# Two more weight parts of the second feed-forward layer by adding transfers, and three more turns of zeros at the start

## The chip, the cores and the metric

The kernel runs on one core of a Trainium2 chip. A core has a matrix engine (TensorE, PE in the profile, with its weight loads as PEld), a vector engine (VectorE, DVE), a scalar engine (ScalarE, ACT), a general engine (GpSimd, POOL) and a sync engine (SyncE, SP) that here only issues transfers. Each engine takes its instructions in the order in which they were written, and waits for other engines at semaphores. The metric is the device time of one execution in microseconds.

## The reference

One residual block over 512 positions of width 1024, all in float32:

```python
h = h + 0.5 * _swiglu(_rmsnorm(h, ffn1_norm[i]), ffn1_w_in[i], ffn1_w_out[i])
z = _rmsnorm(h, mix_norm[i]) @ w_in[i]
...
h = h + jnp.concatenate([y_conv, y_gla], axis=-1) @ w_out[i]
h = h + 0.5 * _swiglu(_rmsnorm(h, ffn2_norm[i]), ffn2_w_in[i], ffn2_w_out[i])
gate = jax.nn.sigmoid(_rmsnorm(h, ple_norm[i]) @ ple_w_gate[i])
h = h + gate * (p[i] @ ple_w_proj[i])
```

`_swiglu` splits `x @ w_in` into a gate and an up half, 2816 columns each, and returns `(silu(gate) * up) @ w_out`. The change lies in the second of these feed-forward layers, and in the first microseconds of the program.

## The kernel before

Activations are kept transposed, as tiles of 128 features by 512 positions. Every float32 product is made of three products of a shorter format: each operand is split into a high part (a cast, names that end in H, or wh for weights) and a lesser part, what the cast left out (names in L, or wl). PE then computes high by high, high by lesser and lesser by high into one bank of PSUM.

**How a weight tile gets its two parts.** A load of 512 KB, issued by SP, fills one of six raw buffers (wr). Then `high` (line 183) casts it on ACT into wh. The lesser part is made in one of two ways. `low` (line 193) is one subtraction on DVE, wl = wr - wh. `added` (line 198) leaves DVE out: ACT copies the tile with a factor of -1 into wl, and POOL issues a transfer that adds wr to it. What is written as `p.part(name)` is `high` and `low`; `p.add_part(name)` is `high` and `added`, where wl first takes minus the high part:

```python
        h3, l3, r3 = w
        act.mul(l3, r3, -1.0)
        pool.dma_start(out=l3.bitcast(F32), in_=r3, accum_op=ALU.add)
```

The profile's row for the multiplication is an ACT ACTIVATE `wl<-wr`, and for the transfer a POOL DMA `wl<-wr`. There are six buffers each for wh and wl.

**The feed-forward layer.** `ffn` (line 604) handles the 22 blocks of 128 gate and up columns as eleven pairs. Pair 0 is computed plainly ahead of the layer's plan. For each other pair the 2 by 2 arrangement of its weights (a11, a12, a21, a22) is multiplied in seven products instead of eight, on sums of the weights (s1 to s4, made by DVE) and of the activations (t1 to t4). The seven are the units m1, m2, m6, m7, m5, m4 and m3, each of 24 matmuls of 128x256. A pair's units take the operands a11, a12, s2, s3, s1, a22 and s4 in that order. Several units add into the same bank of PSUM; where one of them needs the sum so far, ACT copies it out first (`snap`, rows `sq<-ps` and `u<-ps`), and the next unit that adds to this bank must wait for the copy. So unit m5 of a pair can only begin once ACT has copied out what m6 left (`p.u2`, row `u<-ps`).

**What sets the order.** The units stand in one list, and `drive` (line 584) goes through it. Each unit has preparations with a distance: a preparation of distance 4 (`AHEAD`) is written four units ahead of the unit that needs it, ahead of that unit's matmuls; loads have 7 or 9. Between the units stand the pieces of the layer's second product with `w_out`. Where the second layer begins, the list reads: m1, m2 of pair 1, m1 of pair 2, then m6, m7, m5 of pair 1, m2 of pair 2, m4 and m3 of pair 1, m6, m7, m5 of pair 2, m1 and m2 of pair 3, a piece of `w_out`, m4 and m3 of pair 2. PE, DVE and ACT are held to the written order here; the gating (bank plus copy, times the row factor, silu on ACT, product on DVE: rows u, g, s, m) is written behind the unit that ends it.

**The start.** `warm_up(n)` (line 140) has PE turn (transpose) the identity n times into a bank that nobody reads; the document calls these turns of zeros after the change's name for them. Ten stand ahead of the turn of the first gain vector (`turn_vec`, row `ax<-ident,vcol1r`), and four between the turn of the first 128 columns of x (`turn_x(0)`, row `ps<-ident,x`) and the first real products (`ps<-hgH,wh`). The spare bank (ax) is a single one: the gain vector's turn waits until the last of the ten has ended, and the four wait until DVE has copied the gain vector out.

Of the kernel before, what the change touches and what calls it, by code (L numbers as in the profile page):

```python
# [62 lines left out]
def block_kernel(ctx: ExitStack, tc: tile.TileContext, a: dict, out: bass.AP):  # L63
# [32 lines left out]
    def bank():  # L96
        return pp.tile([P, SEQ], F32, tag="mm", bufs=7, name=nm("ps"))

    def aux():
        return pp.tile([P, SEQ], F32, tag="aux", bufs=1, name=nm("ax"))  # L100
# [15 lines left out]
    def columns(names, n, tile_name, queue):  # L116

        row = cp.tile([n, P], F32, name=tile_name + "r")
        col = cp.tile([P, n], F32, name=tile_name)
        r0 = 0  # L120
        for name, m in names:
            queue.dma_start(out=row[r0:r0 + m, :], in_=a[name][0].rearrange("(r p) -> r p", p=P))
            for c in range(m):
                vcols[name, c] = col[:, r0 + c:r0 + c + 1]
            r0 += m

        def turn():
            ps = aux()
            pe.transpose(ps[:, 0:n], row, ident[:n, :n])
            dve.tensor_copy(col, ps[:, 0:n])  # L130

        return turn
# [7 lines left out]
    def warm_up(n):  # L140
        idle = aux()
        for _ in range(n):
            pe.transpose(idle[:, 0:P], ident, ident)

    warm_up(10)
    turn_vec = columns(vecs[:1], 8, "vcol1", nc.scalar)

    def split(src, s, alloc=bt):
# [110 lines left out]
    def spread(col, copy=True):  # L259

        ps = aux()
        for j in range(TB):
            pe.transpose(ps[:, j * P:(j + 1) * P], col[:, j:j + 1].to_broadcast([P, P]), ident)
        if not copy:
            return ps
        bc = tmp("bc", bufs=1)
        act.copy(bc, ps)
        return bc
# [170 lines left out]
    hg, xps, xt, squares = [], [], {}, []  # L439
# [12 lines left out]
    def turn_x(c):  # L452
        ps = bank()
        for t in range(TB):
            pe.transpose(ps[:, t * P:(t + 1) * P], xt[c][t], ident)
        xps.append(ps)
# [63 lines left out]
        nc.sync.dma_start(out=made[2][i * RANK:(i + 1) * RANK, :], in_=a["gate_w_up"][0])  # L520
    turn_vec()
    turn_x(0)
    warm_up(4)
    ps0 = [bank() for _ in range(4)]
    split_w(0, 1, dve.tensor_copy)
    split_x(0)
    mid = []
# [22 lines left out]
    xb = Right(hg, "ffn1_norm")  # L550
# [31 lines left out]
    AHEAD = 4  # L582
# [18 lines left out]
        for f in left:  # L601
            f()

    def ffn(w_in, w_out, x, gname, given, first, rsb, hooks, plain):


        norm = Norm()
# [93 lines left out]
        def plain_unit(j):  # L701

            up, i, k = j // 4, j // 2 % 2, j % 2
            def run(p):
                if not j:
                    p.g, p.s = {}, {}
                if not k:
                    p.x = bank()
                ps = p.x
                wh, wl = p.part(f"a{1 + up}{1 + k}")  # L710
                cs = slice(i * P, (i + 1) * P)
                for c in range(4):
                    mm3(ps, wh[:, c, cs], wl[:, c, cs], *x.rows[4 * k + c], k == c == 0, k == 1 and c == 3)
                if not k:
                    return []
                if not up:
                    def gate():
                        p.s[i] = silu(scaled(ps, "g1"))
                    return [gate]
                return [lambda: gated_block(p, p.s[i], scaled(ps, "u1"), i),  # L720
                        lambda: act_parts(p) if i else None]
            return run
# [4 lines left out]
        def unit(kind, i):  # L727
            p = pairs[i]

            def go(run):  # L730
                left = run(p)
                hooks.get((kind, i), lambda *_: None)()
                return left

            if kind[0] == "h":
                j = int(kind[1])
                part, run = (f"a{1 + j // 4}{1 + j % 2}", plain_unit(j)) if j % 4 < 2 else (None, plain_unit(j))
                if part:
                    return [(AHEAD, lambda: p.part(part)), (9, lambda: p.fetch(part))], lambda: go(run)
            else:  # L740
                part, run = USES[kind]
            before = [(AHEAD + (kind == 'm5'), lambda: p.part(part))] if part else []
            if kind in ("m1", "m2"):
                before.append((7, lambda: p.fetch(part)))
            elif kind == "m6":
                before += [(9, lambda: p.fetch("a21", "a22")), (6, p.s12)]
            elif kind in ("m7", "m3"):
                before.append((6, p.s3_ if kind == "m7" else p.s4_))

            return before, lambda: go(run)  # L750
# [63 lines left out]
        def add(kind, i):  # L814
            if 0 <= i < npair and (kind, i) not in had:
                had.add((kind, i))
                units.append(unit(kind, i))
# [49 lines left out]
    w_in = a["w_in"][0]  # L867
    w_ahead = []

    def sums_hooks(x, names, at):  # L870

        h = {}
        for name, key in zip(names, at):
            h[key] = lambda *_, name=name: x.split(name)
        return h

    hooks = sums_hooks(xb, ("t2", "t3", "t1", "t4"), (("h5", 1), ("h7", 1), ("h3", 2), ("m1", 3)))
    hooks.update({("h%d" % (i + 1), 1): f for i, f in enumerate(steps[2:])})
    hooks.update({("m5", 3): lambda *_: made[0](), ("m5", 4): lambda *_: constants(),
                  ("m4", 10): lambda *_: w_ahead.append(ahead(w_in, D_CONV, 2 * P)),  # L880
                  ("last", 4): lambda *_: w_ahead.append(ahead(w_in, 0, 2 * P))})
    hg, norm = ffn(ffn1_in, a["ffn1_w_out"][0], xb, "mix_norm", {0: Left(ffn1_in, 0), 1: w1},
                   (ps0[:2], ps0[2:]), lambda: spread(mid[0]), hooks, (1, 2))
    pool.on = False
# [63 lines left out]
    mid = []  # L948
# [10 lines left out]
    rs, rsb = mid  # L959
# [358 lines left out]
    ffn2_in = a["ffn2_w_in"][0]  # L1318
    wf = {i: Left(ffn2_in, 2 * i) for i in range(3)}
# [41 lines left out]
    norm = Norm()  # L1361
# [57 lines left out]
    hg = nhg  # L1419

    def plain_block(p, up, i, mid={}):
        ps = bank()
        cs = slice(i * P, (i + 1) * P)
        for k in range(DC):
            if k in mid:
                mid[k]()
            wh, wl = p.part(f"a{1 + up}{1 + k // 4}")
            mm3(ps, wh[:, k % 4, cs], wl[:, k % 4, cs], *hg[k], k == 0, k == DC - 1)
        return ps

    mid = []
    xb = Right(hg, "ffn2_norm")
# [5 lines left out]
    g0 = plain_block(w0, 0, 0)  # L1438
    steps[1]()
    steps[2]()  # L1440
    u0 = plain_block(w0, 1, 0, {4: lambda: mid.append(norm.rows())})
# [4 lines left out]
    g1_ = plain_block(w0, 0, 1, {1: lambda: mid.append(spread(mid[0]))})  # L1446
# [5 lines left out]
    u1_ = plain_block(w0, 1, 1)  # L1452
# [3 lines left out]
    hooks = sums_hooks(xb, ("t4",), (("m2", 1),))  # L1456
# [63 lines left out]
    def todo(*fs):  # L1520
        return lambda *_: [f(*v) for f, *v in fs]
# [4 lines left out]
                  ("rest", 2): todo((q_high, b21, q21, 0), (first_sum, 0), (third_sum, 0)),  # L1526
                  ("rest", 4): todo((q_high, b21, q21, 1), (first_sum, 1), (third_sum, 1)),
                  ("rest", 6): todo((final_in,), (row_sums, 0))})
    hg, norm = ffn(ffn2_in, a["ffn2_w_out"][0], xb, "ple_norm", wf, ((g0, u0), (g1_, u1_)), mid[1], hooks, ())

# [143 lines left out]
    def kept(ps, name, **kw):  # L1676
        o = tmp(name, **kw)
        act.copy(o, ps)
        return o
# [23 lines left out]
    m1 = [kept(p_, "sq", bufs=3) for p_ in x_]  # L1703
# [98 lines left out]
```

## Time and profile before

| | us |
|---|---|
| median of three runs | 949.27 |
| the three runs | 949.77, 949.27, 948.17 |
| the profiled execution | 948.38 |
| its span, first to last instruction | 946.7 |
| PE busy in the span | 935.0 (99%) |
| DVE busy | 755.6 (80%) |
| ACT busy | 477.0 (50%) |
| POOL busy | 57.2 (6%) |

The span lies inside the profiled execution; 1.7 us of it are outside the first and last instruction. Starts in the rows are counted from the span's start. A row of the timeline gives start, duration, engine, line, operation, tiles and shapes, how many equal instructions follow each other, and in brackets the engine's idle time just ahead and what ended it. The line is nearly always L46, a helper that records every operation, so rows are told apart by their tiles; buffer numbers are left out there. Matmuls overlap: each is shown with 0.28 us or more, but they follow each other at a shorter distance, and it is this distance that counts.

In the second layer PE goes through a unit in 2.88 us, one matmul every 0.12 us. Before the change m6 of pair 2 starts at 586.23, m7 at 589.11, m5 at 593.10, m1 of pair 3 at 596.07, m2 of pair 3 at 598.95 and m4 of pair 2 at 607.30.

### The profile page before, as it was taken

What the parts mean: (1) busy time and instruction counts of PE and PEld (TensorE: products, weight loads), DVE (VectorE), ACT (ScalarE), POOL (GpSimd) and SP (SyncE); (2) the same over time, 40 slices, a digit from 0 to 9 for tenths busy, and PEclk for the clock granted to TensorE, in tenths of its full rate; (3) what the DMA queues carried; (4) which work ended last, traced back from release to release, by engine and by line L of the source; (5) the groups of instructions that cost most, each with busy time, mean ns of one, the idle gap of its engine ahead of it and who ended that gap; (6) DMA issues with size and microseconds to landing.
All of it is one profiled execution on the core that took longest, in us unless ns stands there. A gap on an engine that the chain in (4) does not pass through costs nothing.

```text
span 946.7 us, 14553 instructions
## 1 busy us (share of the span) xinstructions
PE 935.0 (99%) x5842; PEld 831.1 (88%) x5842; DVE 755.6 (80%) x1030; ACT 477.0 (50%) x720; POOL 57.2 (6%) x72
## 2 busy tenths in 40 slices
PE   9999999999999999999999999999999999999996
PEld 7888999999999988788877889899999999998885
DVE  5876887887788566999986788887878787866896
ACT  5652544434433574463564874444434433445882
POOL 0000200000000110001030020000000000000121
PEclk9999999999999999999999999999999999999998
DMA  7532323342323593346552572332243224347463
GB/s 229 180 114 72 106 69 117 105 131 80 103 90 111 140 257 83 81 102 167 134 126 77 154 163 82 112 114 88 90 134 112 67 91 133 96 147 225 89 113 110
DMA packets 107831, 113.43 MB, mean 120 GB/s; under 512 B 5155, under 2 KB 96469, under 8 KB 107764
## 3 DMA queue, kind: packets, MB, share of 16 engines
q1 hardware_dynamic: 101732, 94.67, 32.3%
q0 software_dynamic: 6016, 17.83, 10.4%
q8 instruction: 46, 0.75, 0.3%
q14 instruction: 21, 0.17, 0.1%
q10 hardware_dynamic: 16, 0.00, 0.0%
HBM read 93.61 MB, written 2.10 MB: 101 GB/s over the span
## 4 chain that ended last, share of the span: by engine, by line
PE 96%; DVE 2%; ACT 1%; issue 1%; POOLq 0%; POOL 0%; DVEq 0%; ACTq 0%
PE ps L46 94%; PE ax L46 2%; DVE wl L46 1%; DVE g L46 0%; ACT wh L46 0%; DVE u L46 0%; DVE wr L46 0%; ACT s L46 0%; DVE y L46 0%; DVE sm L46 0%; DVE actL L46 0%; DVE hgL L46 0%; ACT wl L46 0%; POOLq L1798 0%; ACT ycH L46 0%
## 5 line engine op out<-in xcount | busy, mean ns | idle before, releaser
L46 PE MATMUL ps<-hgH,wh 128*128 128x256 f32 (+1 forms) x768 | 235.9, 312 | 0.0
L46 PE MATMUL ps<-hgL,wh 128*128 128x256 f32 (+1 forms) x768 | 234.2, 310 | 0.0
L46 PE MATMUL ps<-hgH,wl 128*128 128x256 f32 (+1 forms) x768 | 234.0, 310 | 0.0
L46 DVE TENSOR_TENSOR wl<-wr,wh 128x1024 fp32r<-128x1024 f32 (+2 forms) x162 | 189.6, 1181 | 48.1 <-ACT wh L46 48.0
L46 ACT CAST wh<-wr 128x1024 fp32r<-128x1024 f32 (+2 forms) x177 | 177.8, 1019 | 39.8 <-PE ps L46 19.8
L46 PEld LDWEIGHTS ps<-hgH,wh 128*128 128x128 f32 x768 | 146.9, 192 | 9.9 <-issue 1.1
L46 PEld LDWEIGHTS ps<-hgH,wl 128*128 128x128 f32 x768 | 146.7, 191 | 7.8
L46 PEld LDWEIGHTS ps<-hgL,wh 128*128 128x128 f32 x768 | 146.3, 191 | 8.0 <-issue 0.2
L46 PE MATMUL ps<-actH,wh 128*128 128x512 f32 x352 | 137.4, 390 | 0.0
L46 PE MATMUL ps<-actL,wh 128*128 128x512 f32 x352 | 137.3, 390 | 0.0
L46 PE MATMUL ps<-actH,wl 128*128 128x512 f32 x352 | 136.9, 389 | 0.0
L46 ACT ACTIVATE s<-g 128x512 f32<-128x512 f32 x48 | 30.4, 633 | 190.2 <-DVE g L46 190.2
L46 DVE SCALAR_TENSOR_TENSOR cv<-glu,cw,cv 128x502 f32<-128x502 f32 (+24 forms) x120 | 81.0, 731 | 0.6
L46 PEld LDWEIGHTS ps<-actH,wl 128*128 128x128 f32 x352 | 66.1, 188 | 14.0
L46 PEld LDWEIGHTS ps<-actH,wh 128*128 128x128 f32 x352 | 66.2, 188 | 13.0
L46 PEld LDWEIGHTS ps<-actL,wh 128*128 128x128 f32 x352 | 66.2, 188 | 12.4
L46 DVE SCALAR_TENSOR_TENSOR h<-ps,h 128x512 f32<-128x512 f32 x80 | 53.9, 686 | 21.3 <-PE ps L46 21.2
L46 ACT COPY sq<-ps 128x512 f32<-128x512 f32 x40 | 23.3, 585 | 68.4 <-PE ps L46 68.3
L46 DVE TENSOR_TENSOR wl<-sm,wh 128x1024 fp32r<-128x1024 f32 x40 | 48.7, 1221 | 5.1 <-ACT wh L46 4.9
L46 ACT CAST wh<-sm 128x1024 fp32r<-128x1024 f32 x40 | 41.7, 1043 | 7.0 <-DVE sm L46 4.2
L46 ACT CAST actH<-m 128x512 fp32r<-128x512 f32 x44 | 25.4, 618 | 38.5 <-DVE m L46 38.4
L46 PE MATMUL ps<-t1H,wh 128*128 128x256 f32 x144 | 40.9, 284 | 1.0 <-ACT u L46 1.0
(267 smaller groups left out, 1744.2 us busy)
## 6 DMA issues: line engine op xcount, KB each, us to landing
wr<-in_ffn_w_in SPq DMA_DIRECT2D x84, 512.0 KB
wr<-in_ffn_w_out SPq DMA_DIRECT2D x32, 512.0 KB
wr<-in_w_in SPq DMA_DIRECT2D x20, 512.0 KB
wl<-wr POOLq DMA_DIRECT2D x16, 512.0 KB, 5.5
wr<-in_ffn_w_out SPq DMA_DIRECT2D x16, 384.0 KB
wr<-in_w_out SPq DMA_DIRECT2D x8, 512.0 KB
wq<-in_ple_w_gate SPq DMA_DIRECT2D x8, 512.0 KB
wl<-wq POOLq DMA_DIRECT2D x8, 512.0 KB, 5.3
```

The source lines that it names most:

```text
L46: inst = call(*args, **kwargs)
```

## The change

The unit m4 of pair 2 and the unit m1 of pair 3 of the second layer get their weights by `add_part` instead of `part`, at a distance of 6 units instead of 4. So a22 of pair 2 and a11 of pair 3 lose a subtraction on DVE each, and gain a multiplication on ACT and a transfer issued by POOL; and both their casts on ACT move two units forward in the written order. At the start, the ten turns of zeros become eleven and the four become six.

```diff
-    warm_up(10)
+    warm_up(11)
...
-    warm_up(4)
+    warm_up(6)
...
-    def ffn(w_in, w_out, x, gname, given, first, rsb, hooks, plain):
+    def ffn(w_in, w_out, x, gname, given, first, rsb, hooks, plain, adds=()):
...
-            before = [(AHEAD + (kind == 'm5'), lambda: p.part(part))] if part else []
+            if (kind, i) in adds:
+                before = [(AHEAD + 2, lambda: p.add_part(part))]
+            else:
+                before = [(AHEAD + (kind == 'm5'), lambda: p.part(part))] if part else []
...
-    hg, norm = ffn(ffn2_in, a["ffn2_w_out"][0], xb, "ple_norm", wf, ((g0, u0), (g1_, u1_)), mid[1], hooks, ())
+    hg, norm = ffn(ffn2_in, a["ffn2_w_out"][0], xb, "ple_norm", wf, ((g0, u0), (g1_, u1_)), mid[1], hooks, (), {("m4", 2), ("m1", 3)})
```

**ACT, around unit m6 of pair 2.** The rows are in the order in which ACT takes them, with buffer numbers kept; the last number of a name differs by 3 or a little more between the two programs, because three turns were added. Before: `s_988` is a silu of pair 1, `wh_990` and `wh_992` the casts of s1 and s3 of pair 2, `s_997` a silu of pair 2, `wh_1000` the cast of a11 of pair 3, `s_1003` the last silu of pair 1, `wh_1006` the cast of a12 of pair 3, and `u2_1008` the copy for which m5 of pair 2 waits.

```order
L46 ACTIVATE s_988_5703<-g1_987_5700 128x512
L46 COPY wh_990_5707<-sm_976_5605 128x1024
L46 COPY wh_992_5711<-wr_963_5501 128x1024
L46 ACTIVATE s_997_5745<-g1_996_5742 128x512
L46 COPY wh_1000_5776<-wr_982_5665 128x1024
L46 ACTIVATE s_1003_5806<-g1_1002_5804 128x512
L46 COPY wh_1006_5812<-wr_989_5705 128x1024
L46 COPY u2_1008_5841<-ps_974_5578 128x512
```

After, with the same first and last instruction, `wh_990` and `wl_991` belong to a11 of pair 3, `wh_992` and `wh_994` are the casts of s1 and s3, `wh_1006` and `wl_1007` belong to a22 of pair 2, and `wh_1008` is the cast of a12 of pair 3:

```order
L46 ACTIVATE s_988_5706<-g1_987_5703 128x512
L46 COPY wh_990_5710<-wr_982_5668 128x1024
L46 ACTIVATE wl_991_5711<-wr_982_5668 128x1024
L46 COPY wh_992_5715<-sm_976_5608 128x1024
L46 COPY wh_994_5719<-wr_963_5504 128x1024
L46 ACTIVATE s_999_5753<-g1_998_5750 128x512
L46 ACTIVATE s_1003_5810<-g1_1002_5808 128x512
L46 COPY wh_1006_5816<-wr_964_5506 128x1024
L46 ACTIVATE wl_1007_5817<-wr_964_5506 128x1024
L46 COPY wh_1008_5821<-wr_989_5708 128x1024
L46 COPY u2_1010_5850<-ps_974_5581 128x512
```

Between the two ends stand nine instructions instead of six: the two of a11 of pair 3 have moved ahead of the casts of s1 and s3, and the two of a22 of pair 2, whose cast stood behind the copy, now stand ahead of it.

**DVE, at the same place.** Before, `wl_1001` is the subtraction of a11 of pair 3; it stands ahead of `g1_1002`, from which ACT makes the silu `s_1003`.

```order
L46 TENSOR_TENSOR g1_996_5742<-g1_996_5742,bc_931_5389 128x512
L46 TENSOR_TENSOR u1_998_5771<-ps_981_5640,u2_978_5633 128x512
L46 TENSOR_TENSOR u1_998_5771<-u1_998_5771,bc_931_5389 128x512
L46 TENSOR_TENSOR m_999_5774<-u1_998_5771,s_988_5703 128x2x256
L46 TENSOR_TENSOR wl_1001_5777<-wr_982_5665,wh_1000_5776 128x1024
L46 TENSOR_TENSOR g1_1002_5804<-ps_967_5509,bc_931_5389 128x512
```

After:

```order
L46 TENSOR_TENSOR g1_998_5750<-g1_998_5750,bc_931_5392 128x512
L46 TENSOR_TENSOR u1_1000_5779<-ps_981_5643,u2_978_5636 128x512
L46 TENSOR_TENSOR u1_1000_5779<-u1_1000_5779,bc_931_5392 128x512
L46 TENSOR_TENSOR m_1001_5782<-u1_1000_5779,s_988_5706 128x2x256
L46 TENSOR_TENSOR g1_1002_5808<-ps_967_5512,bc_931_5392 128x512
```

The subtraction is gone, and `g1_1002` follows the product m at once. The subtraction of a22 of pair 2, further on, is gone as well.

**PE, at the start.** Before:

```order
L46 MATMUL ax_1_81<-ident_70 128x128 x10
L46 MATMUL ax_27_161<-ident_70,vcol1r_92 128x8
L46 MATMUL ps_28_164<-ident_70,x_15_108 128x128 x4
L46 MATMUL ax_29_169<-ident_70 128x128 x4
L46 MATMUL ps_30_174<-hgH_36_182,wh_34_178 128x512
```

After:

```order
L46 MATMUL ax_1_81<-ident_70 128x128 x11
L46 MATMUL ax_27_162<-ident_70,vcol1r_93 128x8
L46 MATMUL ps_28_165<-ident_70,x_15_109 128x128 x4
L46 MATMUL ax_29_170<-ident_70 128x128 x6
L46 MATMUL ps_30_177<-hgH_36_185,wh_34_181 128x512
```

Only the two counts differ. Elsewhere every engine's order is the same in both programs; SP's is the same throughout.

## The prediction

> **What bounds the kernel now.** I read the page first, then PE's waits in the second layer, then the timelines of ACT and DVE around the one wait that they show, and last the windows of the granted clock.
>
> ```profile
> PE 935.0 (99%) x5842; PEld 831.1 (88%) x5842; DVE 755.6 (80%) x1030; ACT 477.0 (50%) x720; POOL 57.2 (6%) x72
> ```
>
> PE is the bound: of 946.7 us it is idle for 11.7. An engine beside it, however loaded, costs time only where PE waits for it. In the stretch that the change touches (560 to 640 us) PE's waits are these two:
>
> ```profile
> PE ps L46 <- ACT u L46: 1.0, 1, 1.0
> PE ps L46 <- ACT sq L46: 0.2, 1, 0.2
> ```
>
> The long one stands at the start of m5 of pair 2 (rows with t1H), which may not add to its bank before ACT has copied out what m6 left:
>
> ```profile
> 591.87 0.28 PE L46 MATMUL ps<-t3H,wl 128*128 128x256 f32 x1
> 593.10 0.39 PE L46 MATMUL ps<-t1H,wh 128*128 128x256 f32 x1 [0.95 <-ACT u L46]
> ```
>
> At its usual distance of 0.12 us the matmul would have started at 591.99, so the stall is 1.11 us. m6 had ended at 589.1; the copy was late because ACT got to it late. ACT there, in its order:
>
> ```profile
> 581.82 0.63 ACT L46 ACTIVATE s<-g 128x512 f32<-128x512 f32 x1 [3.44 <-DVE g L46]
> 582.36 1.03 ACT L46 CAST wh<-sm 128x1024 fp32r<-128x1024 f32 x1
> 583.30 1.04 ACT L46 CAST wh<-wr 128x1024 fp32r<-128x1024 f32 x1
> 587.15 0.63 ACT L46 ACTIVATE s<-g 128x512 f32<-128x512 f32 x1 [2.81 <-DVE g L46]
> 587.68 1.03 ACT L46 CAST wh<-wr 128x1024 fp32r<-128x1024 f32 x1
> 591.00 0.63 ACT L46 ACTIVATE s<-g 128x512 f32<-128x512 f32 x1 [2.28 <-DVE g L46]
> 591.53 1.03 ACT L46 CAST wh<-wr 128x1024 fp32r<-128x1024 f32 x1
> 592.47 0.58 ACT L46 COPY u<-ps 128x512 f32<-128x512 f32 x1
> ```
>
> The reader should see that ACT is half idle here and yet late. Each silu (s) waits for DVE's g, and everything written behind it waits too: at 591.00 a silu is released by DVE, then come one cast and the copy. DVE in turn:
>
> ```profile
> 581.03 0.69 DVE L46 TENSOR_TENSOR g<-g,bc 128x512 f32<-128x512 f32 x1
> 583.42 1.23 DVE L46 TENSOR_TENSOR wl<-sm,wh 128x1024 fp32r<-128x1024 f32 x1 [1.70 <-ACT wh L46]
> 584.57 1.22 DVE L46 TENSOR_TENSOR wl<-wr,wh 128x1024 fp32r<-128x1024 f32 x1
> 585.70 0.68 DVE L46 TENSOR_TENSOR g<-ps,sq 128x512 f32<-128x512 f32 x1
> 586.42 0.69 DVE L46 TENSOR_TENSOR g<-g,bc 128x512 f32<-128x512 f32 x1
> ...
> 588.47 0.69 DVE L46 TENSOR_TENSOR m<-u,s 128x512 f32<-128x512 f32 x1
> 589.08 1.22 DVE L46 TENSOR_TENSOR wl<-wr,wh 128x1024 fp32r<-128x1024 f32 x1
> 590.22 0.68 DVE L46 TENSOR_TENSOR g<-ps,bc 128x512 f32<-128x512 f32 x1
> ```
>
> It waits 1.70 us for ACT's cast of s1, and from there runs without a gap to the g of 590.22. So the stall hangs on a chain that goes back and forth: ACT's casts of s1 and s3, DVE's work to 590.22, ACT's silu, cast and copy.
>
> **The change on that chain.** Whatever is put on ACT ahead of the casts of s1 and s3, or between the last silu and the copy, lengthens it. The change does both. The price of a cast with its multiplication on ACT, from where three such stand in a row:
>
> ```profile
> 552.82 1.05 ACT L46 CAST wh<-wr 128x1024 fp32r<-128x1024 f32 x1
> 553.77 1.05 ACT L46 ACTIVATE wl<-wr 128x1024 fp32r<-128x1024 f32 x1
> 554.73 1.03 ACT L46 CAST wh<-wr 128x1024 fp32r<-128x1024 f32 x1
> ```
>
> A cast is followed after 0.95, a multiplication after 0.96; the pair takes 1.91 us. Now step by step.
>
> 1. ACT's silu of 581.82 stays. Behind it come a11's cast and multiplication (pair 3), and the cast of s1 starts at 582.36 + 1.91 = 584.27, that of s3 at 585.21. Its operand is there: of the two loads below, issued back to back, the second is a11's.
>
> ```profile
> 562.78 0.92 SPq L176 DMA_DIRECT2D wr<-in_ffn_w_in  x2
> ```
>
> 2. DVE's first wl starts 1.06 behind the start of the cast it needs (583.42 against 582.36), so now at 585.33, and the whole run to m shifts by 1.91: m starts at 590.38.
> 3. The wl of 589.08 (a11) is gone. The last g follows m after 0.61, as that wl did, and starts at 590.99 instead of 590.22. The subtraction saved 1.14 us, the two instructions ahead cost 1.91: the relief of DVE is more than spent, + 0.77.
> 4. ACT's last silu comes 0.78 behind g (591.00 against 590.22), at 591.77, and the next instruction 0.53 later, at 592.30. There stand now a22's cast and multiplication (1.91), then the cast of a12 that was there before (0.94), then the copy, at 595.15 instead of 592.47.
> 5. PE goes on 0.63 behind the copy's start (593.10 against 592.47), at 595.78. The stall grows from 1.11 to 3.79 us: **+2.7 us**, from 0.77 on DVE's way and 1.91 ahead of the copy.
>
> The second subtraction that is saved (a22, 1.14 us on DVE) stands behind the copy and releases nobody who is late. Behind the stall all other work moves up against PE: the load that DVE waited for before,
>
> ```profile
> 602.38 1.23 DVE L46 TENSOR_TENSOR sm<-wr,wr 128x1024 f32<-128x1024 f32 x1 [1.25 <-DMA wr<-in_ffn_w_in]
> ```
>
> now waits for the transfer of a22 to give up its buffer. That transfer is issued at about 594.6 and lands 5.5 us later by the row below, so the load starts near 600.2 instead of 598.7, 1.5 us later, while PE is 2.7 later. I cost it at nothing, and if it came over 1.2 us later still, the sums of pair 3 would be as late as before. The added transfers themselves are needed by m1 of pair 3 (596.07, issue about 584.6) and m4 of pair 2 (607.30): both have five or more microseconds in hand. They queue on POOL, which has nothing else to do there.
>
> ```profile
> wl<-wr POOLq DMA_DIRECT2D x16, 512.0 KB, 5.5
> ```
>
> The casts moved forward also take another rotation of the wh and wl buffers, but each new owner follows a unit that PE has left by then: nothing. (The cast of s3, at 585.2, follows m2 of pair 2, which ended two units of 2.88 us before 586.23, where m6 starts; that of a12, at 594.2, follows m3 of pair 1, which ended at 586.23.)
>
> **The clock behind the stall.** A gap of 3.6 us on PE is longer than any in this profile but the start and the end. The end shows what the clock does then; PE's last matmul is over at 938.03:
>
> ```profile
> 939.00:940.00 1.00, 0.00 (x0) 0.00 (x0) 0.90 (x4) 0.16 (x1) 0.00 (x0) 1.00 0.00 0
> 940.00:941.00 1.00, 0.00 (x0) 0.00 (x0) 0.78 (x2) 0.00 (x0) 0.74 (x1) 0.50 0.68 262
> ...
> 591.00:595.00 4.00, 3.05 (x26) 2.85 (x25) 1.83 (x2) 2.59 (x5) 0.00 (x0) 1.00 0.02 4
> ```
>
> Two microseconds after the last matmul the granted clock (third figure from the right) is halved; the stall of before, 0.95 us idle, did not halve it. With 3.6 us idle I expect the half clock when m5 starts. How long it lasts is bounded by the start, where PE is slow until 8.07:
>
> ```profile
> 1.61 2.40 PE L46 MATMUL ax<-ident 128*128 128x128 f32 x10 [1.61 <-POOL ident masks.py:199]
> 4.06 0.18 PEld L46 LDWEIGHTS ax<-ident,vcol1r 8*128 8x128 f32 x1 [0.46 <-PE ax L46]
> 4.96 0.87 PEld L46 LDWEIGHTS ax<-ident 128*128 128x128 f32 x4
> 5.17 1.06 PE L46 MATMUL ax<-ident 128*128 128x128 f32 x4
> 5.42 0.69 ACT L46 ACTIVATE hgH<-ps,vcol 128x512 fp32r<-128x512 f32 x1 [2.49 <-PE ps L46]
> 6.20 1.36 PEld L46 LDWEIGHTS ps<-hgH,wh 128*128 128x128 f32 x4 [0.36 <-ACT hgH L46]
> 6.22 2.05 PE L46 MATMUL ps<-hgH,wh 128*128 128x512 f32 x4
> 8.07 1.15 PE L46 MATMUL ps<-hgH,wl 128*128 128x512 f32 x4
> ```
>
> Four matmuls start between 6.22 and 8.07, 0.46 us apart; the next four take 1.15 us to the end of the last, which is shown with 0.39, so they are 0.25 apart. That is about half the speed before 8.07 and full speed after (the granted clock is given as 1.00 there all the same, so ahead of its first change the record doesn't tell). The slow time lasts at least 1.85 us of real matmuls and at most 6.46 us from the first turn; at half speed half of it is lost, 0.9 to 3.2 us. I take 2.8 us slow and a loss of **1.4**, nearer the lower end, since m5 follows on real work without pauses.
>
> **The turns at the start.** The ten are 0.22 us apart, and the gain vector's turn waits for the last to end (0.46 idle on PEld). An eleventh moves it, the turns of x and ACT's hgH by 0.22: hgH ends at 6.33 instead of 6.11. The six can begin at 4.96 + 0.22 = 5.18 and hold PE for 6 x 0.22 = 1.32, to 6.50: the first product starts about 0.28 later. Of the idle 0.36 they fill all, and overshoot. If the slow time ends at the same moment, the 0.28 slow microseconds are worth 0.14 of fast work; if it moves along, 0.28. The gain is bounded by the slow products: were all of 6.22 to 8.07 fast, 0.9 us. I take **+0.2**, nearer the rows of what is added. [...]
>
> **The sum.** 2.7 + 1.4 + 0.2 = 4.3 us. The profiled execution took 948.38 (1.7 of it outside its span), so 952.7; the median of the runs shown is 0.9 above it, 949.27, which gives **953.5 us**.
>
> **The rivals.**
>
> - *The stall, but no half clock.* The idle 3.6 us might not be enough, if the clock is tested at intervals and finds work on both sides. For it: 0.95 us idle did nothing. Against it: at the end 1.97 sufficed. 949.27 + 2.7 + 0.2 = 952.1. Chance 0.2. [...]
> - *A long slow time.* If the full clock takes the whole 6.46 us to return, 949.27 + 2.7 + 3.2 + 0.2 = 955.4. It is the far end of the forecast and shares its chance.
> - *The stall, hidden by the start.* If the filled gaps bring the full clock before the first product (-0.9) and no half clock follows, 949.27 + 2.7 - 0.9 = 951.1, within 0.2%. 0.2% is 1.9 us, about what a measurement of this kernel can tell from no change. Chance 0.1.
> - *Faster: DVE's relief ends the stall.* This one mechanism would have ACT do a11's cast and multiplication in its idle 3.44 us ahead of 581.82. Then casts and DVE keep their times, the last g comes 1.14 us earlier, and if a22's two are absorbed likewise in the idle 2.28, the copy at 591.3 ends PE's wait: 949.27 - 1.1 = 948.2, with the start's -0.9 at best 947.3. It decides at whether ACT gets to these four before the silus they stand behind; it takes its instructions in order, so it can't. Chance 0.05.
>
> **How the numbers follow.** Forecast 0.65 at 953.5. Its own range is 952.0 to 955.4: below, a loss of 0.9, no cost of the turns and the profiled execution's level (948.38 + 2.7 + 0.9 = 952.0). Together: slower by over 0.2% 0.85, within 0.2% 0.1, faster 0.05. The range 951.2 to 955.5 leaves out the two last rivals and a little of the long slow time; its lower end is the second rival at the profiled execution's level (948.38 + 2.9).
>
> **What would show it.** m5 of pair 2 starts on PE 3.6 to 3.8 us after m7's last matmul, released by ACT's u; ACT's copy stands about 3.4 us behind its last silu; DVE waits about 3.6 us, not 1.70, ahead of the wl of s1; the granted clock falls below 1.00 at about 594 to 599 and matmuls are 0.2 us or more apart for some microseconds; no other wait appears between 600 and 640. I am wrong if ACT's copy is on time or if PE's gap is filled by other work.

## The result, and the profile after

The changed kernel takes 952.52 us (median of 7 runs, 950.11 to 953.28), the kernel before 948.41 (7 runs beside them, 947.44 to 949.77). The ratio is 1.0038, with a 95% interval of 1.0026 to 1.005: slower by 2.5 to 4.7 us. The profiled execution took 952.28, 3.90 us more than that of before, with a span of 950.6.

The first part of the page, the busy times:

```profile
PE 936.4 (99%) x5845; PEld 833.0 (88%) x5845; DVE 753.4 (79%) x1028; ACT 479.0 (50%) x722; POOL 58.8 (6%) x74
```

DVE has its two subtractions less, ACT and POOL their two instructions more. PE is busy for only 1.4 us more, so most of the 3.9 is idle time. Of PE's waits this is the one that answers to the long one of before:

```profile
PE ps L46 <- ACT u L46: 3.6, 1, 3.6
```

It is the same wait as before, 1.0 then and 3.6 now. PE's timeline around it, the last matmul of m7 and the first two of m5 of pair 2:

```profile
592.00 0.28 PE L46 MATMUL ps<-t3H,wl 128*128 128x256 f32 x1
595.86 0.58 PE L46 MATMUL ps<-t1H,wh 128*128 128x256 f32 x1 [3.59 <-ACT u L46]
596.24 0.41 PE L46 MATMUL ps<-t1L,wh 128*128 128x256 f32 x1
```

Two things are to be seen: a stall of 595.86 - 592.12 = 3.74 us (1.11 before), and the distance of the two matmuls behind it, 0.38 instead of 0.12. ACT's timeline tells where the stall is from:

```profile
581.94 0.63 ACT L46 ACTIVATE s<-g 128x512 f32<-128x512 f32 x1 [3.43 <-DVE g L46]
582.48 1.03 ACT L46 CAST wh<-wr 128x1024 fp32r<-128x1024 f32 x1
583.41 1.05 ACT L46 ACTIVATE wl<-wr 128x1024 fp32r<-128x1024 f32 x1
584.37 1.03 ACT L46 CAST wh<-sm 128x1024 fp32r<-128x1024 f32 x1
585.30 1.05 ACT L46 CAST wh<-wr 128x1024 fp32r<-128x1024 f32 x1
...
591.87 0.63 ACT L46 ACTIVATE s<-g 128x512 f32<-128x512 f32 x1 [2.08 <-DVE g L46]
592.41 1.03 ACT L46 CAST wh<-wr 128x1024 fp32r<-128x1024 f32 x1
593.34 1.05 ACT L46 ACTIVATE wl<-wr 128x1024 fp32r<-128x1024 f32 x1
594.30 1.03 ACT L46 CAST wh<-wr 128x1024 fp32r<-128x1024 f32 x1
595.24 0.57 ACT L46 COPY u<-ps 128x512 f32<-128x512 f32 x1
```

The cast and the multiplication of a11 (582.48, 583.41) stand ahead of the casts of s1 and s3, those of a22 (592.41, 593.34) ahead of the copy. DVE, between them, in its timeline:

```profile
585.43 1.23 DVE L46 TENSOR_TENSOR wl<-sm,wh 128x1024 fp32r<-128x1024 f32 x1 [3.59 <-ACT wh L46]
...
590.49 0.69 DVE L46 TENSOR_TENSOR m<-u,s 128x512 f32<-128x512 f32 x1
591.09 0.68 DVE L46 TENSOR_TENSOR g<-ps,bc 128x512 f32<-128x512 f32 x1
...
603.13 1.22 DVE L46 TENSOR_TENSOR sm<-wr,wr 128x1024 f32<-128x1024 f32 x1 [0.36 <-DMA wr<-in_ffn_w_in]
```

It waits 3.59 us for the cast of s1 (1.70 before). Without the subtraction between m and g the run that follows is one instruction shorter, yet g comes 0.87 later than the 590.22 of before.

The windows of 2 us (busy time and instructions of PE, PEld, DVE, ACT and POOL, then the granted clock, DMA share and GB/s) show the rest:

```profile
592.00:594.00 2.00, 0.28 (x3) 0.07 (x1) 0.00 (x0) 2.00 (x3) 0.00 (x0) 1.00 0.00 0
594.00:596.00 2.00, 0.14 (x1) 0.14 (x1) 0.64 (x1) 1.81 (x3) 0.86 (x1) 0.83 0.00 0
596.00:598.00 2.00, 2.00 (x10) 2.00 (x11) 1.32 (x3) 0.78 (x2) 0.00 (x0) 0.50 1.02 197
598.00:600.00 2.00, 2.00 (x16) 2.00 (x16) 2.00 (x3) 1.31 (x2) 0.00 (x0) 0.82 0.40 74
600.00:602.00 2.00, 2.00 (x19) 2.00 (x18) 2.00 (x3) 1.54 (x2) 0.00 (x0) 1.00 0.59 172
```

PE is idle while ACT works without a pause. The granted clock falls to a half at about 595.3 and is whole again at about 598.7; PE then does 10 matmuls in 2 us instead of 19. From the start of m5 to the first matmul of the piece of `w_out` behind m2 of pair 3 there are 9.98 us now (595.86 to 605.84), against 8.73 before (593.10 to 601.83): the half clock costs 1.25 us.

So the 3.90 us are: 0.13 ahead of m6 of pair 2 (586.36 against 586.23), 2.63 of longer stall, 1.25 of half clock, and 0.1 given back behind it.

The start, in PE's timeline (the six turns and the first products):

```profile
5.38 1.49 PE L46 MATMUL ax<-ident 128*128 128x128 f32 x6
6.52 1.95 PE L46 MATMUL ps<-hgH,wh 128*128 128x512 f32 x4
8.31 1.09 PE L46 MATMUL ps<-hgH,wl 128*128 128x512 f32 x4
```

The first product starts at 6.52 instead of 6.22, and PE becomes fast at about 8.2, as before.

### The profile page after: what moved, and what is told of

Same layout as the page of the kernel before. It is cut to its first block, busy times and chain, and to the rows that moved or that the text cites. A ratio compares the mean times of both kernels' runs of the same rounds, so it can differ in the third digit from the quotient of the medians.

```text
span 950.6 us, 14565 instructions
## 1 busy us (share of the span) xinstructions
PE 936.4 (99%) x5845; PEld 833.0 (88%) x5845; DVE 753.4 (79%) x1028; ACT 479.0 (50%) x722; POOL 58.8 (6%) x74
## 4 chain that ended last, share of the span: by engine, by line
PE 97%; DVE 1%; ACT 1%; issue 0%; POOLq 0%; POOL 0%; ACTq 0%
PE ps L46 96%; PE ax L46 2%; DVE g L46 0%; ACT wh L46 0%; ACT wl L46 0%; DVE u L46 0%; DVE y L46 0%; DVE wl L46 0%; ACT s L46 0%; POOLq L1801 0%; ACT ycH L46 0%; DVE m L46 0%; DVE yc L46 0%; DVE rs L46 0%; ACT sq L46 0%
## 5 line engine op out<-in xcount | busy, mean ns | idle before, releaser
L46 DVE TENSOR_TENSOR wl<-wr,wh 128x1024 fp32r<-128x1024 f32 (+2 forms) x160 | 187.1, 1180 | 50.4 <-ACT wh L46 50.3
```

The source lines that it names most:

```text
L46: inst = call(*args, **kwargs)
```

## The experiments

All kernels compute the whole reference. Diffs are against the kernel before where nothing else is said; "the two sums" are those of a11 of pair 3 and a22 of pair 2. Each run has its own measurement of the kernel before beside it, to which its ratio refers. To compare the traces, three distances are read in each: the stall ahead of m5 of pair 2 (the start of m5 less that of m7, less 2.88), the time from the start of m5 to the piece of `w_out` (8.73 at full clock), and the start of m6, which collects what happened earlier. These three are from one profiled execution of each kernel; the ratio is that of the medians.

| kernel | ratio to before (95%) | m6 starts | stall | half clock costs |
|---|---|---|---|---|
| before | 1 | 586.23 | 1.11 | 0 |
| changed | 1.0038 (1.0026 to 1.005) | 586.36 | 3.74 | 1.25 |
| three turns alone | 1.0003 (0.9994 to 1.0012) | 585.47 | 1.09 | 0 |
| two sums alone | 1.0048 (1.0034 to 1.0062) | 586.14 | 3.74 | 2.70 |
| a22's sum alone | 1.0032 (1.0021 to 1.0044) | 585.37 | 2.98 | 0 |
| a11's sum alone | 1.0014 (1.0005 to 1.0022) | 585.38 | 1.85 | 0 |
| two sums, gap filled with turns | 1.0032 (1.002 to 1.0044) | 585.23 | 3.75 | 0 |
| two sums, gap filled with products | 1.0035 (1.0023 to 1.0048) | 585.89 | 3.75 | 0 |
| no turns at all | 1.0013 (1.0004 to 1.0022) | 586.93 | 1.08 | 0 |
| two sums, planned 5 and 4 units ahead | 1.0023 (1.0014 to 1.0031) | 585.47 | 0 | 0 |
| a11's sum alone, 5 units ahead | 0.9989 (0.998 to 0.9999) | 585.33 | 0 | 0 |
| two sums, both 5 units ahead | 1.0003 (0.9994 to 1.0011) | 587.62 | 0 | 0 |

**The turns alone.**

```diff
-    warm_up(10)
+    warm_up(11)
...
-    warm_up(4)
+    warm_up(6)
```

> Only the three more turns of zeros, no adding transfers. Prediction's theory: the first product starts 0.3 us later (6.5 instead of 6.22), everything behind it 0.13 to 0.3 us later, the stall ahead of m5 of pair 2 stays at 1.1 us; +0.1 to +0.3 us in all. Rival, the turns bring the full clock earlier: up to -0.9 us, and the matmuls of 512 columns become 0.23 us apart before 8 us.

Measured: 947.99 against 947.57. The three turns move the time by less than a measurement can tell. The stall is that of before. The sign of the rival is there in the profile: the first four products of 512 columns start at 6.38 and stand about 0.25 us apart. But in five of the nine profiled executions with the start of before (the kernel before, and those below that leave the turns alone) the first products are as fast, so it does not come from the three turns.

**The two sums alone.**

```diff
+            if (kind, i) in adds:
+                before = [(AHEAD + 2, lambda: p.add_part(part))]
...
-    hg, norm = ffn(..., hooks, ())
+    hg, norm = ffn(..., hooks, (), {("m4", 2), ("m1", 3)})
```

> Only the two adding transfers, the turns as before. Prediction's theory: the stall ahead of m5 of pair 2 is 3.7 us, 2.6 more than before, followed by 3.4 us of half clock that cost 1.2; +3.9 us. Rival, the turns at the start carry a good part of the +4.1: +2 us or less here.

Measured: 953.32 against 947.57. All of the loss is in the two sums. The stall is 3.74 as with the turns, but the half clock lasts twice as long (from 595.0 to 601.8) and costs 2.70 instead of 1.25.

**One sum alone.** The same diff with `{("m4", 2)}` for a22 and with `{("m1", 3)}` for a11.

> Only a22 of pair 2 by an adding transfer at distance 6; a11 of pair 3 as before. Prediction's theory: cast and multiplication stand between ACT's last silu and the copy, 1.91 us; that silu stays at 591.0; stall 1.11 + 1.91 = 3.0 us, and with 2.9 us idle the half clock in most executions; +1.9 us without it, +3 with it. Rival, each adding transfer costs the same wherever it stands: half of the two together, +2 us, with the stall at 2.4.

> Only a11 of pair 3 by an adding transfer at distance 6; a22 of pair 2 as before. Prediction's theory: casts of s1 and s3 1.91 us later, DVE's subtraction saved 1.14, so the silu 0.77 later and the stall 1.9 us; with 1.7 us idle the clock may stay full; +0.8 us, with a half clock +2. Rival, each adding transfer costs the same wherever it stands: +2 us, with the stall at 2.4.

Measured: 951.12 with a22's, 948.85 with a11's, against 947.57. The first matmul of m5 in PE's timeline, with a22's sum:

```profile
594.11 0.39 PE L46 MATMUL ps<-t1H,wh 128*128 128x256 f32 x1 [2.83 <-ACT u L46]
```

With a11's the same wait is 1.69 us.

The stall grows by 1.87 with a22's sum and by 0.74 with a11's; together 2.61, and both at once gave 2.63. So the two ways add up: a22's cast and multiplication ahead of the copy, and a11's ahead of the casts of s1 and s3 less the subtraction. Neither profile shows a half clock, though PE was idle for 2.83 us in the one. With a22's sum the profiled execution, 949.28, was the fastest of six; the others took 950.8 to 951.8. There are no traces of them, but their mean granted clock is on record: 0.994 to 0.996, against 0.998 in the profiled one. So the half clock that the expectation named for most executions very likely did come in them.

**The gap filled.** If the half clock is from PE's idle time, work that nobody needs must prevent it. Added to the two sums:

```diff
+    def fill(*_):
+        idle = aux()
+        for _ in range(26):
+            pe.transpose(idle[:, 0:P], ident, ident)
+
+    hooks[("m7", 2)] = fill
```

and, in case turns and products should differ in this, in a second kernel 25 products instead:

```diff
+        w, xh = wf[2].part("s3")[0], xb.op["t3"][0][0]
+        for _ in range(25):
+            pe.matmul(idle[:, 0:HALF], w[:, 0, 0:P], xh, start=True, stop=True)
```

> Only the two sums by adding transfers (start as before), and 26 turns of the identity matrix into a spare bank of PSUM on TensorE behind the last product of m7 of pair 2, so that TensorE is not idle ahead of m5; their results are not used. With turns at about 0.12 us each they take about 3.1 of the 3.7 us, and m5 cannot start earlier or later for them. Theory A (the loss of 1.25 us at half clock comes from TensorE being idle, and turns count as work): granted clock 1.00 through 592 to 600, and only the stall is left: before + 2.6 us, about 1.3 us less than the two sums without the turns. [...]

> Only the two sums by adding transfers (start as before), and 25 real products of 128x256 (a weight already cast times an activation already there) into a spare bank of PSUM on TensorE behind the last product of m7 of pair 2; their results are not used. At about 0.11 us each they take about 2.8 of the 3.7 us. [...] Theory C (another cause than TensorE's idle time): half clock from about 595 to 598.7 although TensorE works, before + 3.9 us. [...]

Measured: 950.19 with turns and 950.73 with products, against 947.71. PE's timeline with the turns:

```profile
591.00 3.00 PE L46 MATMUL ax<-ident 128*128 128x128 f32 x26
594.74 0.39 PE L46 MATMUL ps<-t1H,wh 128*128 128x256 f32 x1 [0.74 <-ACT u L46]
```

Its windows of 2 us, as above:

```profile
592.00:594.00 2.00, 2.00 (x19) 1.75 (x17) 0.00 (x0) 2.00 (x3) 0.43 (x1) 1.00 0.04 8
594.00:596.00 2.00, 1.26 (x10) 1.26 (x11) 1.76 (x2) 0.69 (x2) 0.43 (x1) 1.00 0.58 113
596.00:598.00 2.00, 2.00 (x19) 2.00 (x18) 1.31 (x4) 1.90 (x3) 0.00 (x0) 1.00 0.80 150
```

m5 starts as late behind m7 as in the changed kernel (6.63 us, 6.62 there), the transfer moves in the same microseconds, and the clock stays whole. With the products it is the same (clock 1.00 from 592 to 600). So the half clock was from PE's idle time, and the 26 turns prevented it as the 25 products did. The ratios alone would not have shown it: their intervals reach from +1.9 to +4.5 us and hold both + 2.6 and + 3.9. The granted clock decides, and not in the two profiles alone: its mean is 0.997 or 0.998 in all eleven timed executions of these two kernels, and 0.994 or 0.995 in the five of the two sums with the gap left open.

**No turns at all.** `warm_up(10)` and `warm_up(4)` are taken out.

> The kernel before without any turns of zeros at the start (all 14 taken away). Theory A (turns count as work for the clock, so that the full clock comes earlier for them): the rise to full clock comes up to 3.4 us later than 8.2 us in the span, up to 1.7 us slower. Theory B (they do not count, and only fill time in which TensorE waits for x): the rise stays at about 8.2 us or moves by less than a few tenths, 0 to 0.3 us faster. With the run that adds three turns (1.0003 of before) this bounds what the part of the change at the start can be worth.

Measured: 949.35 against 947.71, slower by 0.4 to 2.1 us. PE becomes fast between 9.3 and 9.8 in the profiled execution. So the fourteen turns of before are worth 0.4 to 2.1 us, while three more are worth nothing that was measured.

**Both sums, planned later.** The distance is given for each sum; a11's stands then behind ScalarE's casts of s1 and s3, a22's behind the copy.

```diff
+            if (kind, i) in adds:
+                before = [(AHEAD + adds[kind, i], lambda: p.add_part(part))]
...
+    hg, norm = ffn(..., hooks, (), {("m4", 2): 0, ("m1", 3): 1})
```

> Both sums by adding transfers, start as before, but planned later: a11's cast and multiplication are planned five units ahead of its use instead of six, so that they stand behind ScalarE's casts of s1 and s3 and not ahead of them, and a22's four units ahead instead of six, so that they stand behind the copy u. Theory A (the stall grew only because casts and multiplications stand ahead of s1/s3 and of the copy on ScalarE, while the relief of VectorE is real): g is 1.1 us earlier than before, the copy stands at about 591.3, m5 of pair 2 starts with no stall, and the time is before - 1.1 us. [...]

Measured: 950.24 against 947.71. The stall is gone, as expected, but ahead of m5 of pair 3 there is a new one. The chain of work that ended last, with start, duration and what it was:

```profile
596.83 6.74 DMA wl<-wr
...
603.63 3.54 DMA wr<-in_ffn_w_out
...
607.20 1.05 ACT wh L46
```

and its end on PE's timeline:

```profile
624.80 0.39 PE L46 MATMUL ps<-t1H,wh 128*128 128x256 f32 x1 [2.29 <-ACT u L46]
```

The adding transfer held the raw buffer wr until it had landed: issued at 596.83, it took 6.74 us, and the next load of `w_out`, which waited for its buffer, starts at 603.63. In the kernel before, DVE's subtraction of 597.45 was over at 598.67, and the load that waited for it starts at 598.70. The load of `w_out` is issued 12.4 us behind the start of m5 of pair 2, against 5.6 in the changed kernel (601.46 and 595.86). From there ACT's cast, DVE and ACT's copy run late up to the next copy u.

The stall saved and the wait added make 2.45 - 1.11 = 1.3 us, and the profiled execution, 948.94, is 1.2 above the median of before. But seven of the eleven executions took 950.2 to 951.0. Six of these have a mean granted clock of 0.995 or 0.996, the four fastest 0.997, so the new wait too, with its 2.29 us of idle time, seems to have brought the half clock in most of them; no trace shows it.

**a11's sum alone, planned later,** is the same with `{("m1", 3): 1}`.

> Of the run with both sums planned later only a11's is kept (five units ahead, behind ScalarE's casts of s1 and s3); a22's lesser part is subtracted by VectorE as before, and the start is as before. Theory A (what cost in the run with both was a22's transfer alone: issued at 596.83, it held its buffer wr until 603.57, and the next load of w_out came 4.6 us late; a11's transfer costs nothing and saves VectorE 1.14): no stall ahead of m5 of pair 2, none ahead of m5 of pair 3, before - 1.1 us (ratio about 0.9988). Rival D (adding transfers hold their buffers too long in any case): the load behind a11's transfer is late too, a stall of 0.5 to 2.5 us at some unit of pair 3, before or up to 1.4 us slower.

Measured: 947.18 (11 runs, 946.15 to 948.72) against 947.76, 0.1 to 1.9 us faster than the kernel before, and the only kernel here that is. ACT's timeline, from the silu of 580.91 on:

```profile
581.45 1.03 ACT L46 CAST wh<-sm 128x1024 fp32r<-128x1024 f32 x1
582.38 1.99 ACT L46 CAST wh<-wr 128x1024 fp32r<-128x1024 f32 x2
584.28 1.06 ACT L46 ACTIVATE wl<-wr 128x1024 fp32r<-128x1024 f32 x1
586.24 0.63 ACT L46 ACTIVATE s<-g 128x512 f32<-128x512 f32 x1 [0.90 <-DVE g L46]
...
589.49 1.03 ACT L46 CAST wh<-wr 128x1024 fp32r<-128x1024 f32 x1
590.42 0.58 ACT L46 COPY u<-ps 128x512 f32<-128x512 f32 x1
```

PE at the same place:

```profile
590.97 0.28 PE L46 MATMUL ps<-t3H,wl 128*128 128x256 f32 x1
591.09 0.35 PE L46 MATMUL ps<-t1H,wh 128*128 128x256 f32 x1
```

a11's two now stand behind the casts of s1 and s3 and end before the next silu is released. DVE's g comes 1.14 earlier, the copy is on time, and m5 follows m7 at 0.12. No wait takes its place. The whole step is the 1.11 us of the old stall.

**Both sums, five units ahead:** `{("m4", 2): 1, ("m1", 3): 1}`.

> Both sums by adding transfers planned five units ahead, start as before. a22's cast and multiplication stand ahead of the copy u on ScalarE again, so that the transfer goes out about 2 us earlier than in the run with four units and the load of w_out is not late, but the multiplication (0.96) stands ahead of the copy. Theory A: the relief of VectorE (1.14) and the multiplication (0.96) nearly cancel, the stall ahead of m5 of pair 2 is about 0.9 us (before: 1.11) and there is none ahead of m5 of pair 3: before - 0.2 us, no difference that can be measured. Rival D (adding transfers cost of themselves): the wait of 2.3 us ahead of m5 of pair 3 stays, before + 1 to + 2 us.

Measured: 948.28 against 947.76, no difference, as expected, but by other terms. a22's cast and multiplication still stood behind the copy (ACT's copy at 592.72, the multiplication at 596.71), so the stall of pair 2 is gone; and a wait of 1.24 stands ahead of m5 of pair 3 (625.77 there, 4.12 behind the start of m7 instead of 2.88). That is - 1.11 + 1.24. DVE's timeline shows where it is from:

```profile
598.73 1.23 DVE L46 TENSOR_TENSOR wl<-wr,wh 128x1024 fp32r<-128x1024 f32 x1 [0.94 <-ACT wh L46]
604.58 1.23 DVE L46 TENSOR_TENSOR sm<-wr,wr 128x1024 f32<-128x1024 f32 x1 [3.30 <-DMA wr<-in_ffn_w_in]
```

The multiplication stands ahead of a cast on ACT, DVE's wl waits 0.94 for this cast, and the load of `w_in` that takes over DVE's buffer is issued 6.60 us behind the start of m5 instead of 5.60. It is also slower, 4.60 us up to DVE's sum instead of 3.68, with the adding transfer beside it. So the sum starts 11.20 behind m5 instead of 9.28, and from the sum to ACT's copy it is 20.56 us in both kernels. The load of `w_out`, held back by the transfer to 9.5 us behind m5, sets nothing here: DVE's wl that needs it follows without a gap. In the run with five and four units it did, at 12.4.

**The changed kernel twice more,** for two further profiled executions.

> The changed kernel once more, for one more profiled execution. If the time at half clock ahead of and in m5 of pair 2 depends on where the gap lies against the clock's own steps of 3.41 us, it differs between executions of the same program: one step (3.41 us of half clock, a loss of 1.25, as in the changed kernel's profile) or two (6.8 us, a loss of 2.7, as in the profile of the two sums without the turns), and the rise at the start lies anywhere from 5.8 to 8.3 us. If the three turns at the start set it, both are as in the changed kernel's profile: a rise at 8.2 us and a loss of 1.25. The stall is 3.7 us in either case.

> As the run beside it, the changed kernel once more: a stall of 3.7 us, and one or two steps of half clock (a loss of 1.25 or 2.7) if they depend on the execution; one step and a rise at 8.2 us if the turns set it.

Measured: 951.48 and 953.73, beside 947.52 for the kernel before. The windows of the first:

```profile
594.00:596.00 2.00, 1.21 (x9) 1.21 (x10) 1.71 (x2) 0.74 (x2) 0.48 (x1) 0.93 0.50 98
596.00:598.00 2.00, 2.00 (x11) 2.00 (x11) 1.31 (x3) 1.85 (x3) 0.00 (x0) 0.50 0.89 164
598.00:600.00 2.00, 2.00 (x15) 2.00 (x14) 2.00 (x3) 0.78 (x3) 0.00 (x0) 0.72 0.09 21
```

and of the second:

```profile
596.00:598.00 2.00, 2.00 (x10) 2.00 (x11) 1.32 (x3) 0.76 (x2) 0.00 (x0) 0.50 1.02 197
598.00:600.00 2.00, 2.00 (x11) 2.00 (x11) 2.00 (x3) 1.32 (x2) 0.00 (x0) 0.50 0.40 74
600.00:602.00 2.00, 2.00 (x11) 2.00 (x11) 1.45 (x2) 0.60 (x2) 0.00 (x0) 0.50 0.48 132
```

One program, the same stall (3.75 and 3.74), but a half clock of 3.4 us in the first (595.7 to 599.1) and of 6.8 in the second (595.2 to 602.0), costing 1.49 and 2.69. PE's timeline at the start of the first:

```profile
5.30 0.82 PE L46 MATMUL ax<-ident 128*128 128x128 f32 x6
6.25 1.20 PE L46 MATMUL ps<-hgH,wh 128*128 128x512 f32 x4
```

and of the second:

```profile
5.39 1.49 PE L46 MATMUL ax<-ident 128*128 128x128 f32 x6
6.74 1.79 PE L46 MATMUL ps<-hgH,wh 128*128 128x512 f32 x4
```

The six turns take 0.82 us where the clock is whole and 1.49 where it is not: PE became fast at about 5.2 in the one and 8.1 in the other, and reached m6 of pair 2 at 585.28 and 586.37. So the execution, not the three turns, sets when the clock rises and how long it is halved.

## Why the prediction was right

**The stall: right, step by step.** Predicted + 2.7, measured + 2.63. The cast of s1 was put at 584.27 and stood at 584.37, DVE's wl at 585.33 (585.43), g at 590.99 (591.09), the copy at 595.15 (595.24), m5 at 595.78 (595.86). The tenth by which all are later was there already at m6. Its two parts, 0.77 and 1.91, measured 0.74 and 1.87 alone.

**The half clock: right in kind, a little small.** Predicted 1.4 between 0.9 and 3.2. The profiled execution shows 1.25, but four executions with both sums show 1.25, 1.49, 2.69 and 2.70, a mean of 2.0. The step that failed is the reason given for the lower end, that m5 follows on work without pauses: it did in all four, and two lasted two steps. What differs between them is how much of the stall was left behind the fall: in the first step of half clock PE was idle for 0.00 and 0.55 us where one step followed, and for 0.67 and 0.69 where two did. The long slow time, which shared the forecast's chance, came in two of the four at 2.7, not 3.2. None of the four kept the whole clock, but the rival without a half clock very likely did occur: of the seven timed executions of the changed kernel one took 950.11 with a mean granted clock of 0.998 (the others 0.993 to 0.996), 2.67 above the fastest of before beside it, which is about the stall alone. So the median mixes executions with none, one and two steps, and that the sum came this close to it is in part luck.

**The turns: right that they are worth little.** Predicted + 0.2. Alone they gave 1.0003. In the profiled execution the first product came 0.30 later (0.28 predicted) and m6 0.13 later, but that agreement is luck: in the three other executions with these turns the first product starts at 6.25, 6.38 and 6.74, and m6 at 585.28, 585.47 and 586.37, by when the clock rose. Turns did work as products do on the clock here: 26 of them kept it at 1.00 through the gap, and in the first repeated execution PE was fast at 5.3 us after nothing but turns. Whether more turns at the start could bring the full clock earlier was not shown; that these three did not is what was measured.

**The condition for the drop.** The prediction set the drop 1.97 us after the last matmul at the end of the program against the rival without a half clock. In one run PE was not even idle at the drop: in the first repeated execution the clock fell at about 595.7, when PE had been at work again since 594.79, so the 3.41 us ahead of it held some 0.9 us of work. The changed kernel's half clock lasts 3.41 us in its record, and half clocks of that length and of twice that length were seen.

The traces say more about when it falls. In each of the four executions with a half clock the fall behind the stall and the fall at the end of the program are a whole number of steps of 3.413 us apart (595.32 and 946.89 in the changed kernel's profile, 103 steps). Take the same steps in the other traces, counted back from the fall at the end. Then in all fourteen traces the full clock fell at the end of every step in which PE was idle for 1.97 us or more, and of none in which it was idle for 1.84 or less. The profile with a22's sum alone has the 1.84, at its end, and this is how its gap of 2.83 us lies (windows of one step; the second figure is PE's busy time):

```profile
589.33:592.74 3.41, 1.95 (x17) 1.75 (x15) 0.70 (x2) 2.62 (x4) 0.00 (x0) 1.00 0.00 0
592.74:596.15 3.41, 2.04 (x17) 2.04 (x18) 1.85 (x3) 2.00 (x4) 0.86 (x1) 1.00 0.50 96
937.49:940.90 3.41, 1.57 (x14) 1.37 (x12) 3.00 (x13) 1.09 (x2) 0.54 (x1) 1.00 0.01 2
```

A boundary at 592.74 splits it into 1.46 and 1.37, and the clock stays whole. That fits the clock "tested at intervals" with "work on both sides" of the prediction's rival without a half clock. No step had to be idle as a whole, 1.97 of its 3.41 us were enough; and whether a stall like these (2.83 and 3.59 us idle) holds as much in one step depends on where the boundaries fall, which differs between executions: at 595.32, 595.7 and 595.2 in the three profiles of the changed kernel.

**What was costed at nothing.** The transfers are hidden, as said: PE has no other new wait between 600 and 640. The load that DVE waits for was to start 1.5 later; SP's row puts it 0.8 later (599.5 against 598.7), and DVE's wait fell from 1.25 to 0.36. But that the transfer holds the raw buffer can be a real price: planned two units later it cost 2.45. The 1.24 of one unit later are from the multiplication's place on ACT and a slower load.

**The rivals.** The stall hidden by the start did not occur: the turns hid nothing. A full clock ahead of the first product, which it needed, was seen in the first repeated execution, with an m6 0.95 earlier than before, but it was seen with the start of before too. The faster case was rejected since ACT takes its instructions in order, which the trace bears out: with 3.43 us of idle time ahead of the silu of 581.94, a11's cast still came behind it, at 582.48. Its mechanism, DVE's relief, is real nonetheless: with a11's two instructions one unit later it gave the whole 1.1.

**The level.** The sum, 4.3, stood on a median of 949.27; beside the changed kernel the same program took 948.41. Against that the measured 4.1 is 0.2 below the sum. The rest of the miss of 1.0 is the level.

## What to carry to other kernels

Moving work from a busy engine to a half idle one paid here only where the instructions stand behind what others wait for; a11's cast and multiplication cost 0.74 us ahead of two casts and saved 1.1 behind them. A stall on TensorE can cost a half clock as well: in these traces 1.97 us of idle time in one step of 3.41 was the least that did. With 3.6 us idle it came in all four profiled executions, at 1.3 to 2.7 us more, and a stall that can't be removed can be filled with work that nobody needs: 26 turns kept the clock at 1.00. The transfer that adds in place held its source buffer until it landed, 6.74 us in the slowest case here: count which load is waiting for that buffer.

## What the runs showed of the hardware

- The moment at which the clock rises at the start differs between executions of one program: about 5.2 us in one of the changed kernel and 8.1 in another; it was about 10.8 in the run with both sums five units ahead, whose first products still stood 0.46 apart. Among kernels with the same start, m6 of pair 2 begins between 585.23 and 587.62, by and large later where the clock rises later. Comparing two profiled executions, one has to take the start off first.
- The half clock came and went in steps: 3.4 us in two executions with both sums, 6.8 in two others.
- The clock can fall after PE has resumed work (at 595.7, work since 594.79).
- In fourteen traces the clock fell at the end of the steps of 3.41 us in which PE was idle for 1.97 us or more, and stayed with 1.84 or less. So 2.83 us of idle time left it whole in one profiled execution, where a boundary split them, and 3.6 halved it in all four profiled ones. When it rises again is not settled: behind the stall 0.55 us of idle time in a step still let it rise and 0.67 did not.
- An adding transfer of 512 KB took 4.7 and 4.8 us in the changed kernel, 5.1 and 6.7 in the run with both sums planned five and four units ahead. Why the last was slower is not settled; loads moved beside it for a part of the time.
